# Attention scores of two column blocks written in one run of six products into one piece of two PSUM banks

## The chip, the cores and the metric

The kernel runs on one core of one Trainium2 chip. The metric is the device time of one execution in microseconds; the time given for a kernel is the median of its timed runs.

## What is computed

One layer of an encoder with a convolution branch and an attention branch, over 16 meta tokens and two batches of 512 and 1024 tokens, 1024 features, 16 heads of 64. All inputs are fp32. Cut to what matters here:

```python
u = rms_norm(h, pre_g)
z = einsum('bld,de->ble', u, w_in)            # c_val, c_glu, c_gate, q, k, v, a_gate
conv_out = conv_module(c_val, c_glu, ...) * silu(c_gate)
o_meta, o_grid = neighbourhood_attention(q, k, v, ..., rel_bias)
att = concat([o_meta, o_grid]) * silu(a_gate)
y = einsum('ble,ed->bld', concat([conv_out, att]), w_out)
out = h + rms_norm(y, post_g)
```

The attention is over a window: a token grid 64 columns wide is cut into column blocks, and each query sees 8 rows by 16 columns of keys and the meta keys, with a bias for the relative position. Of each query row the kernel computes the scores, adds bias and mask, takes the softmax and the weighted sum of the values.

## The kernel before

Each fp32 operand of a large matrix product is split into a high and a low part (names with h and l, or hi and lo), and a product is made of three: high by high, high by low, low by high.

**Stages.** First `prenorm` and the projections of the values and of the convolution branch, while VectorE runs the convolution taps (L272). Then the attention loop (L687): `groups` holds 8 head pairs `p`, 3 row groups `g` and 2 halves `hf`, 48 in all. One round `n` writes `scores` of group n, `weighted` of group n-2, `transposes` of group n-1 and `between`, which writes projections of the next keys, queries and gates (L180) to go between; `statistics` (L648) reduces the convolution output for a layer norm. Behind the loop stand the gate projections `a_gate(6, 7)` (L707): six groups of 24 products, each copied out of PSUM by ScalarE (L342). Then the last stage, the output projection (`product`, L794), whose inputs come from `mix` (L757): loads, two VectorE passes, ScalarE `Silu` (L770, L771), a product by the gate (L772), and the split into `mh` (L773) and `ml` (L774). The weights of that projection are split by `load_wo` (L748, L749).

**The scores.** `scores` (L565) treats four column blocks `jj`. For each it takes a piece `ss` of PSUM, issues three products into it (L578), and VectorE reads the piece once (L585), adding the bias and taking the maximum. Then come the exponential on ScalarE (L589), a reciprocal and a scaling on VectorE. `transposes` (L600) turns the result on TensorE into `tp`, ScalarE copies it to SBUF (L602), and `weighted` multiplies it with the values (L616) into `po`.

**PSUM.** Eight banks: `ps_mm` has three (projections, tiles `mm`), `ps_s` two (`ss`), `ps_t` two (`tp`), `ps_o` one (`po`). All are closed before the last stage, and `ps_y` (L711) takes all eight (tiles `py`).

**What sets the order.** The kernel is written through a framework that takes the instructions as they are traced and orders them on each engine with a time model of its own, before anything runs; it places tiles in free buffers and puts in the semaphore waits. Three lines hold parts of that order by hand: `weighted` is issued behind the last score product of the round, the last gates behind the last weighted sum, and the first `mix` behind the last transposed copy, scaling and store:

```python
            with tc.issue_after(last_qk[0].ins):
                weighted(*groups[n - 2])
...
    with tc.issue_after(last_pv[0]):
        for _ in a_gate(6, 7):
...
    with tc.issue_after(last_pt[0]), tc.issue_after(last_norm[0]), tc.issue_after(stores[-2]):
        mix(0, (0,))
```

All transfers are issued on one queue, SyncE's.

Of the kernel before, what the change touches and what calls it, by code (L numbers as in the profile page):

```python
# [10 lines left out]
F32 = mybir.dt.float32  # L11
# [21 lines left out]
GR = (  # L33
    dict(R=9, k3=(0, 11, 0), k2=(0, 16, 0), vrow=0),
    dict(R=12, k3=(8, 12, 0), k2=(8, 16, 0), vrow=8),
    dict(R=13, k3=(13, 13, 0), k2=(10, 16, 3), vrow=13),
)
# [40 lines left out]
BMM, BSS, BTP = 3, 2, 2  # L78
# [15 lines left out]
def tile_encoder(ctx: ExitStack, tc: tile.TileContext, mt, xn, w_main, w_v, wo, cw, cb, lg, lb, pg, postg, rbt, rmask, y):  # L94
    nc = tc.nc
# [9 lines left out]
    const = ctx.enter_context(tc.tile_pool(name="const", bufs=1))  # L105
    es_ps = ExitStack()
    ps_mm = es_ps.enter_context(tc.tile_pool(name="ps_mm", bufs=BMM, space=bass.MemoryType.PSUM))
    ps_s = es_ps.enter_context(tc.tile_pool(name="ps_s", bufs=BSS, space=bass.MemoryType.PSUM))
    ps_t = es_ps.enter_context(tc.tile_pool(name="ps_t", bufs=BTP, space=bass.MemoryType.PSUM))
    ps_o = es_ps.enter_context(tc.tile_pool(name="ps_o", bufs=1, space=bass.MemoryType.PSUM))  # L110

    ones = const.tile([128, 128], F32, name="ones")
    nc.vector.memset(ones, 1.0 / D)
# [317 lines left out]


    es2 = ExitStack()
    kpool = es2.enter_context(tc.tile_pool(name="kpool", bufs=1, side="right", reuse_waits="tile"))
    qpool = es2.enter_context(tc.tile_pool(name="qpool", bufs=1, side="right", reuse_waits="tile"))

# [46 lines left out]
    last_qk = [None]  # L483
# [59 lines left out]
    def block(g, j):  # L543

        e = ebufs[g][{0: 1, 7: 2}.get(j, 0)]
        if g == 0:
            return min(max(j - 1, 0), 5), 3, "k3", 2, 108, e
        R8 = GR[g]["R"] * 8
        if j in (0, 7):
            return min(j, 6), 2, "k2", 2, R8, e  # L550
        return j - 1, 3, "k3", 3, R8, e

    def load_values(p, g):
        esl = slice(p * 128, p * 128 + 128)
        R8 = GR[g]["R"] * 8
        if g == 0:
            vt = apool.tile([108, 2, 6, 128], F32, name="vp", bufs=VPB)
            for ch, p0, b0, k0, n in ((0, 0, 0, 0, 72), (0, 72, 1, 0, 36), (1, 0, 1, 36, 36), (1, 36, 2, 0, 72)):
                nc.sync.dma_start(vt[p0:p0 + n, ch], vd[b0:b0 + 6, k0:k0 + n, esl].rearrange("b k e -> k b e"))
        else:  # L560
            vt = apool.tile([104, 8, 128], F32, name="vt", bufs=2)
            nc.sync.dma_start(vt[:R8], vd[:, GR[g]["vrow"] * 8:GR[g]["vrow"] * 8 + R8, esl].rearrange("b k e -> k b e"))
        vts[p, g] = vt

    def scores(p, g, hf):  # L565
        if hf == 0:
            load_values(p, g)
        kh, kl = kbufs[p]
        qh, ql = qbuf.pop((p, g, hf))
        R8 = GR[g]["R"] * 8  # L570
        for jj in range(4):
            j = hf * 4 + jj
            b0, nk, key, _, _, e = block(g, j)
            ra, rn, ro = GR[g][key]
            w = rn * 8
            ss = ps_s.tile([128, 512], F32, name="ss")
            for i, (q, k) in enumerate(((qh, kh), (qh, kl), (ql, kh))):
                last_qk[0] = nc.tensor.matmul(ss[:, :nk * w], lhsT=q[:, jj].rearrange("p h x -> p (h x)"),  # L578
                                 rhs=k[:, b0:b0 + nk, ra:ra + rn, :].rearrange("p b r c -> p b (r c)"),
                                 start=(i == 0), stop=(i == 2))  # L580
            sv_ = ss[:, :nk * w].rearrange("p (k x) -> p k x", k=nk)[:, :, ro * 8:ro * 8 + R8]
            pt = apool.tile([128, 312], F32, name="pt", bufs=PTB)
            pv = pt[:, :nk * R8]
            sm = apool.tile([128, 4], F32, name="sm", bufs=8)
            nc.vector.tensor_tensor_reduce(out=pv.rearrange("p (k x) -> p k x", k=nk), in0=sv_,  # L585
                                           in1=e.rearrange("p k r c -> p k (r c)"), scale=1.0,
                                           scalar=-3.0e38, op0=ALU.add, op1=ALU.max, accum_out=sm[:, 0:1])
            nc.vector.tensor_scalar(out=sm[:, 1:2], in0=sm[:, 0:1], scalar1=-1.0, scalar2=None, op0=ALU.mult)  # L588
            last[0] = nc.scalar.activation(out=pv, in_=pv, func=AF.Exp, bias=sm[:, 1:2], scale=1.0, accum_out=sm[:, 2:3])  # L589
            nc.vector.reciprocal(sm[:, 3:4], sm[:, 2:3])  # L590
            last_norm[0] = nc.vector.tensor_scalar(out=pv, in0=pv, scalar1=sm[:, 3:4], scalar2=None, op0=ALU.mult).ins  # L591
            pts[p, g, j] = pv
# [94 lines left out]
    for n in range(len(groups) + 2):  # L687
        if n < len(groups):
            p, g, hf = groups[n]
            if (g, hf) == (0, 0) and p > 0:  # L690
                e_build(p)
            scores(p, g, hf)
        if n == len(groups) + 1:
            next(rest)
        if n >= 2:
            with tc.issue_after(last_qk[0].ins):
                weighted(*groups[n - 2])
        if n == len(groups):
            next(rest)
        if 0 <= n - 1 < len(groups):  # L700
            transposes(*groups[n - 1])
        if n < len(groups):
            between(p, g * 2 + hf)
        if n >= STAT0:
            next(stats, None)
# [206 lines left out]
```

## Time and profile before

| | |
|---|---|
| timed runs | 1452.44, 1453.23, 1454.35 us; median 1453.23 |
| the profiled execution | 1453.64 us, of which the span from first to last instruction is 1451.4 |
| TensorE busy | 1434.7 us, 99% of the span |
| VectorE, ScalarE, GpSimdE busy | 70%, 39%, 18% |
| chain of waits that ended last | TensorE 96% |
| attention loop (first score product to the last gates) | 647.7 to 1143.9 us of the span |
| last gates; output projection | 1143.9 to 1177.0; 1177.0 to 1445.4 us |

TensorE's rows in the timeline overlap, since products are pipelined and their ends are modelled. The time that a product takes is read from the start of its row to the start of the next one, not from the duration in the row.

### The profile page before, as it was taken

The page shows a single profiled execution, that of the slowest core. Times are in us where ns is not written, and L with a number is a line of the kernel's source. Part 1 is how long each engine was busy: PE and PEld are TensorE (multiplying, and loading weights), DVE is VectorE, ACT ScalarE, POOL GpSimd, SP SyncE. Part 2 cuts the span into 40 slices and gives each one's busy share as a digit, 9 for nine tenths or more (in the row PEclk, how much of TensorE's full clock was granted, in tenths as well). Part 3 has the DMA queues.
Part 4 walks back from the last instruction along what each step waited for, and adds up shares of the span by engine and source line. Part 5 has one row for each costly group of instructions (what it writes and reads, how often), then busy time and mean ns, then how long its engine had stood idle before and what let it go on. Part 6 is the DMA issues. An engine that isn't in the chain of part 4 may idle for free.

```text
span 1451.4 us, 24134 instructions
## 1 busy us (share of the span) xinstructions
PE 1434.7 (99%) x9536; PEld 1238.8 (85%) x9536; DVE 1012.5 (70%) x1739; ACT 563.5 (39%) x1299; POOL 255.8 (18%) x188
## 2 busy tenths in 40 slices
PE   7999999999999999999999999999999999999998
PEld 6988998988998888888888888888888888888886
DVE  5699999998999899935776677777644373423331
ACT  7312111111111111135555555555554475445540
POOL 2042013102111221121111111111201002221220
PEclk9999999999999999999999999999999999999999
DMA  8113213312231222251232323322332684545441
GB/s 265 47 42 113 59 54 113 90 44 82 84 94 41 77 76 91 80 139 46 74 99 73 90 80 90 95 66 84 80 68 75 206 285 133 166 128 161 131 131 50
DMA packets 153464, 145.19 MB, mean 100 GB/s; under 512 B 37216, under 2 KB 125432, under 8 KB 153352
## 3 DMA queue, kind: packets, MB, share of 16 engines
q1 hardware_dynamic: 153352, 143.67, 33.1%
q8 instruction: 74, 1.21, 0.4%
q14 instruction: 38, 0.31, 0.1%
HBM read 105.35 MB, written 42.72 MB: 102 GB/s over the span
## 4 chain that ended last, share of the span: by engine, by line
PE 96%; POOL 1%; DVE 1%; DMA 1%; ACT 1%; issue 0%; DVEq 0%; SPq 0%; ACTq 0%; POOLq 0%
PE mm L180 39%; PE py L794 18%; PE tp L180 9%; PE mm L322 6%; PE ss L578 5%; PE po L180 5%; PE po L616 4%; PE tp L600 4%; PE tp L322 3%; POOL vl L142 1%; PE po L322 1%; PE ss L202 0%; DMA gb<-in_pg 0%; PE tp L202 0%; PE mm L664 0%; DMA wraw<-in_w_main 0%
## 5 line engine op out<-in xcount | busy, mean ns | idle before, releaser
L180 PE MATMUL mm<-uw,whi 128*128 128x512 f32 (+2 forms) x1904 | 559.8, 371 | 0.0
L272 DVE SCALAR_TENSOR_TENSOR z<-ub,cw_sb,z 128x1536 f32<-128x1536 f32 (+2 forms) x270 | 498.7, 1854 | 8.1
L180 PEld LDWEIGHTS mm<-uw,whi 128*128 128x128 f32 x1904 | 341.8, 188 | 55.2 <-issue 1.3
L180 PE MATMUL mm<-uw,wlo 128*128 128x512 f32 (+2 forms) x952 | 352.3, 370 | 1.1 <-POOL wlo L142 1.1
L142 POOL TENSOR_TENSOR wlo<-wraw,whi 128x1024 fp32r<-128x1024 f32 x48 | 129.5, 2699 | 526.5 <-ACT whi L141 502.7
L180 PEld LDWEIGHTS mm<-uw,wlo 128*128 128x128 f32 x952 | 179.0, 188 | 27.3 <-POOL wlo L142 1.4
L794 PE MATMUL py<-uw,mh 128*128 128x512 f32 x576 | 180.9, 395 | 0.0
L180 PE MATMUL tp<-uw,whi 128*128 128x512 f32 (+2 forms) x512 | 132.9, 344 | 0.0
L794 PEld LDWEIGHTS py<-uw,mh 128*128 128x128 f32 x576 | 108.1, 188 | 25.4
L589 ACT ACTIVATE pt<-pt,sm 128x216 f32<-128x216 f32 (+4 forms) x192 | 97.3, 507 | 80.1 <-DVE sm L588 70.8
L794 PE MATMUL py<-uw,ml 128*128 128x512 f32 x288 | 113.3, 394 | 0.0
L602 ACT COPY pT<-tp 108x256 f32<-108x256 f32 (+4 forms) x192 | 78.2, 420 | 83.8 <-PE tp L600 52.6
L767 DVE TENSOR_TENSOR mx<-mx,mb 128x1024 f32<-128x1024 f32 x12 | 16.1, 1340 | 120.8 <-DMA mx<-zs 120.8
L180 PEld LDWEIGHTS tp<-uw,whi 128*128 128x128 f32 x512 | 89.3, 188 | 11.6
L585 DVE CUSTOM_DVE_ANT_0 pt<-ss,ei 128x216 f32<-128x216 f32 (+2 forms) x144 | 62.6, 437 | 45.4 <-PE ss L578 22.9
L180 PE MATMUL tp<-uw,wlo 128*128 128x512 f32 (+2 forms) x256 | 88.1, 344 | 0.0
L774 POOL TENSOR_TENSOR ml<-mx,mh 128x1024 fp32r<-128x1024 f32 x20 | 48.5, 2441 | 216.4 <-ACT mh L773 216.4
L600 PE MATMUL tp<-ident,pt 128*96 128x128 f32 (+2 forms) x480 | 85.5, 275 | 0.3 <-ACT pT L602 0.2
L322 PE MATMUL mm<-vh,uw 128*128 128x256 f32 x448 | 84.6, 289 | 0.2 <-ACT uw L205 0.2
L591 DVE TENSOR_SCALAR pt<-pt,sm 128x216 f32<-128x216 f32 (+4 forms) x192 | 71.7, 373 | 4.9
L141 ACT CAST whi<-wraw 128x1024 fp32r<-128x1024 f32 x48 | 50.3, 1047 | 61.1 <-DMA wraw<-in_w_main 18.6
L180 PE MATMUL po<-uw,whi 128*128 128x512 f32 (+2 forms) x272 | 72.9, 347 | 0.0
(170 smaller groups left out, 2174.0 us busy)
## 6 DMA issues: line engine op xcount, KB each, us to landing
wraw<-in_w_main SPq DMA_DIRECT2D x48, 512.0 KB
xt<-in_xn SPq DMA_DIRECT2D x12, 512.0 KB
vd<-vs SPq DMA_DIRECT2D x96, 64.0 KB
zs<-zc SPq DMA_DIRECT2D x24, 256.0 KB
cgd<-ag SPq DMA_DIRECT2D x24, 256.0 KB
agd<-ag SPq DMA_DIRECT2D x24, 256.0 KB
ag<-zs SPq DMA_DIRECT2D x24, 256.0 KB
mad<-mo SPq DMA_DIRECT2D x24, 256.0 KB
```

What stands on the lines that cost most here:

```text
L142: eng.tensor_tensor(out=lo, in0=raw, in1=hi.bitcast(F32), op=ALU.subtract)
L180: last_mm[0] = nc.tensor.matmul(ps[:, :n], lhsT=w[:, dc, :], rhs=u[dc // 4][:, dc % 4, :], start=(dc == 0 and i == 0), stop=(dc == DC - 1 ...
L272: nc.vector.scalar_tensor_tensor(out=zv, in0=ub[:, a:b, k:k + 512], scalar=cw_sb[:, c, k:k + 1], in1=zv, op0=ALU.mult, op1=ALU.add)
L322: nc.tensor.matmul(ps[:, :256], lhsT=u[dc // 4][:, dc % 4, :], rhs=w[dc // 4][:, dc % 4, :], start=(dc == 0 and i == 0), stop=(dc == DC - ...
L578: last_qk[0] = nc.tensor.matmul(ss[:, :nk * w], lhsT=q[:, jj].rearrange("p h x -> p (h x)"), rhs=k[:, b0:b0 + nk, ra:ra + rn, :].rearrange ...
L585: nc.vector.tensor_tensor_reduce(out=pv.rearrange("p (k x) -> p k x", k=nk), in0=sv_, in1=e.rearrange("p k r c -> p k (r c)"), scale=1.0, ...
L589: last[0] = nc.scalar.activation(out=pv, in_=pv, func=AF.Exp, bias=sm[:, 1:2], scale=1.0, accum_out=sm[:, 2:3])
L591: last_norm[0] = nc.vector.tensor_scalar(out=pv, in0=pv, scalar1=sm[:, 3:4], scalar2=None, op0=ALU.mult).ins
L600: nc.tensor.transpose(out=tp[:kt, k * 128:k * 128 + 128], in_=pv[:, k * kt:k * kt + kt], identity=ident)
L602: last_pt[0] = nc.scalar.copy(out=pT[:kt, :nt * 128], in_=tp[:kt, :nt * 128]).ins
L616: last_pv[0] = nc.tensor.matmul(po[hs, j, :], lhsT=v, rhs=pT[:kt, k * 128 + h * 64:k * 128 + h * 64 + 64], start=(k == 0), stop=(k == nt - ...
L794: nc.tensor.matmul(pss[hf], lhsT=m[e // 8][:, e % 8], rhs=w[e][:, hf * 512:hf * 512 + 512], start=(n == 0 and i == 0), stop=(n == 15 and i ...
```

## The change

The six products of two neighbouring column blocks are issued together into one tile `sss` of two banks, and each half is then read by VectorE as before. The number and the shapes of the products stay the same, and so do all other instructions. The pool of `ss` is opened last, so that it can be closed behind the first stages, and its two banks become the one piece of the new pool `ps_ss`. Line numbers behind the edit move by up to 8: L578 is L582, L600 is L608, L616 is L624, L794 is L802 and so on.

```diff
     ps_mm = es_ps.enter_context(tc.tile_pool(name="ps_mm", bufs=BMM, space=bass.MemoryType.PSUM))
-    ps_s = es_ps.enter_context(tc.tile_pool(name="ps_s", bufs=BSS, space=bass.MemoryType.PSUM))
     ps_t = es_ps.enter_context(tc.tile_pool(name="ps_t", bufs=BTP, space=bass.MemoryType.PSUM))
     ps_o = es_ps.enter_context(tc.tile_pool(name="ps_o", bufs=1, space=bass.MemoryType.PSUM))
+    es_st = ExitStack()
+    ps_s = es_st.enter_context(tc.tile_pool(name="ps_s", bufs=BSS, space=bass.MemoryType.PSUM, reuse_waits="tile"))
...
     es2 = ExitStack()
+    es_st.close()
+    ps_ss = es_ps.enter_context(tc.tile_pool(name="ps_ss", bufs=1, space=bass.MemoryType.PSUM, reuse_waits="tile"))
...
         for jj in range(4):
             j = hf * 4 + jj
+            if jj % 2 == 0:
+                sss = ps_ss.tile([128, 2, 512], F32, name="sss")
+                for y in range(2):
+                    b0, nk, key, _, _, e = block(g, j + y)
+                    ra, rn, ro = GR[g][key]
+                    for i, (q, k) in enumerate(((qh, kh), (qh, kl), (ql, kh))):
+                        last_qk[0] = nc.tensor.matmul(sss[:, y, :nk * rn * 8], lhsT=q[:, jj + y].rearrange("p h x -> p (h x)"),
+                                                      rhs=k[:, b0:b0 + nk, ra:ra + rn, :].rearrange("p b r c -> p b (r c)"),
+                                                      start=(i == 0), stop=(i == 2))
             b0, nk, key, _, _, e = block(g, j)
             ra, rn, ro = GR[g][key]
             w = rn * 8
-            ss = ps_s.tile([128, 512], F32, name="ss")
-            for i, (q, k) in enumerate(((qh, kh), (qh, kl), (ql, kh))):
-                last_qk[0] = nc.tensor.matmul(ss[:, :nk * w], lhsT=q[:, jj].rearrange("p h x -> p (h x)"),
-                                 rhs=k[:, b0:b0 + nk, ra:ra + rn, :].rearrange("p b r c -> p b (r c)"),
-                                 start=(i == 0), stop=(i == 2))
+            ss = sss[:, jj % 2]
```

The framework orders the changed program anew. Up to the first score product TensorE's order is the same. Behind it the rows move on every engine. Three places:

TensorE in the attention loop, before, at a border of two rounds (tiles: `ss` scores, `po` weighted sums, `tp` transposes, `mm` projections):

```order
L578 MATMUL ss<-kh,ql_5181 128x256
L616 MATMUL po<-pT,vp 64x64 x16
L600 MATMUL tp<-ident,pt 96x128
L578 MATMUL ss<-kh,qh_5186 128x256
L578 MATMUL ss<-kl,qh_5186 128x256
L578 MATMUL ss<-kh,ql_5187 128x256
L180 MATMUL mm<-uw,whi 128x512
L180 MATMUL mm<-uw,wlo 128x512
```

The same round after the change, from the second product of its first block of columns on (`ones` is the small product of `statistics`):

```order
L582 MATMUL sss<-kl,qh_5190 128x256
L582 MATMUL sss<-kh,ql_5191 128x256
L582 MATMUL sss<-kh,qh_5190 128x312
L608 MATMUL tp<-ident,pt 96x128 x3
L582 MATMUL sss<-kl,qh_5190 128x312
L582 MATMUL sss<-kh,ql_5191 128x312
L181 MATMUL mm<-uw,whi 128x512
L181 MATMUL mm<-uw,wlo 128x512
L181 MATMUL mm<-uw,whi 128x512
L672 MATMUL mm<-cw_sb,ones 128x128
L608 MATMUL tp<-ident,pt 96x128 x6
L582 MATMUL sss<-kh,qh_5190 128x312
```

Before, a round's first three products stood alone behind the weighted sums. Now two blocks stand together, here with three transposes between, and the next run of six needs the same piece of PSUM after three projection products, one small product and six transposes.

ScalarE at the end of the last gates, before: from the last six `Silu` passes over the first convolution input to the copy of the sixth and last gate product (`gt` gates, `uw` weights of the output projection, `ag` gate copies; DMAHW are the transfers' semaphores):

```order
L770 ACTIVATE mx<-mx,lb_sb,lg_sb 128x128 x6
L771 ACTIVATE gt<-gt 128x1024 [waits DMAHW1_49]
L748 CAST uw<-xr 128x1024
L748 CAST uw<-yo 128x1024
L773 CAST mh_12158<-mx_12153 128x1024 [waits DVE_49]
L748 CAST uw<-wraw 128x1024 [waits DMAHW4_49]
L771 ACTIVATE gt_12154<-gt_12154 128x1024 [waits DMAHW5_49]
L342 COPY ag<-mm 128x512 [waits DMAHW1_49,PE_49,Activation_49]
L748 CAST uw<-wraw 128x1024 [waits DMAHW7_49]
L773 CAST mh_12159<-mx 128x1024 [waits DVE_49]
L771 ACTIVATE gt<-gt 128x1024 [waits DMAHW0_49]
L342 COPY ag<-mm 128x512 [waits DMAHW6_49,PE_49]
```

The same stretch after the change; ahead of it stand the copy of the fourth gate product and the eight passes of L778:

```order
L779 ACTIVATE gt<-gt 128x1024
L779 ACTIVATE gt_12062<-gt_12062 128x1024 [waits DMAHW1_49]
L756 CAST uw<-wraw 128x1024 [waits DMAHW3_49]
L756 CAST uw<-xr 128x1024
L756 CAST uw<-yo 128x1024
L756 CAST uw<-wraw 128x1024 [waits DMAHW4_49]
L343 COPY ag<-mm 128x512 [waits DMAHW0_49,PE_49,Activation_49]
L781 CAST mh_12067<-mx 128x1024 [waits DVE_49]
L781 CAST mh_12066<-mx_12061 128x1024 [waits DVE_49]
L779 ACTIVATE gt<-gt 128x1024 [waits DMAHW6_49]
L779 ACTIVATE gt_12062<-gt_12062 128x1024 [waits DMAHW7_49]
L343 COPY ag<-mm 128x512 [waits DMAHW5_49,PE_49]
```

In both orders the copy of the last gate product is the last row, with the same kinds of passes ahead of it; now two gate passes that each wait for a transfer stand directly before it.

TensorE at the border of the last gates and the output projection (tile numbers kept), before:

```order
L180 MATMUL mm_12102<-uw_118,wlo_11959 128x512
L180 MATMUL mm_12102<-uw_120,whi_11958 128x512
L794 MATMUL py_12300<-woh0_12184,mh_12148 128x512 [waits Activation_49]
L794 MATMUL py_12300<-wol0_12185,mh_12148 128x512 [waits DVE_49]
L794 MATMUL py_12300<-woh0_12184,ml0_12161 128x512 [waits DVE_49]
```

And after the change:

```order
L181 MATMUL mm_12010<-uw_118,wlo_11867 128x512
L181 MATMUL mm_12010<-uw_120,whi_11866 128x512
L802 MATMUL py_12208<-woh0_12092,mh_12056 128x512 [waits Activation_49]
L802 MATMUL py_12208<-wol0_12093,mh_12056 128x512 [waits DVE_49]
L802 MATMUL py_12208<-woh0_12092,ml0_12069 128x512 [waits DVE_49]
```

The rows are the same, and the places in PSUM are not. In both programs the first output tile (`py_12300`, `py_12208`) lies in bank 0. The six gate products before it take the three banks of `ps_mm` in turn: before the change banks 0, 2, 1, 0, 2, 1, after it 1, 2, 0, 1, 2, 0. So the last user of bank 0 ahead of the first output tile was the fourth gate product, and is now the sixth, `mm_12010`.

## Rows read from the trace of the kernel before

**Rows 1.** The page: span, TensorE's busy time, its granted clock in 40 slices.

```profile
span 1451.4 us, 24134 instructions
PE 1434.7 (99%) x9536; PEld 1238.8 (85%) x9536; DVE 1012.5 (70%) x1739; ACT 563.5 (39%) x1299; POOL 255.8 (18%) x188
...
PEclk9999999999999999999999999999999999999999
```

**Rows 2.** Chain of waits, its two last pieces: start us, us, what.

```profile
1143.93 33.12 PE mm L180 x144
1177.05 268.34 PE py L794 x1152
```

**Rows 3.** Groups by line, VectorE in the attention loop: busy us, mean ns | idle before.

```profile
L585 DVE CUSTOM_DVE_ANT_0 pt<-ss,ei 128x216 f32<-128x216 f32 (+2 forms) x144 | 62.6, 437 | 45.4 <-PE ss L578 22.9 <-PE tp L600 21.2
...
L660 DVE TENSOR_REDUCE cw_sb<-ag 128x64 f32<-128x512 f32 x48 | 51.2, 1078 | 15.2 <-DMA ag<-zs 13.6 <-PE mm L664 1.5
...
L585 DVE DVE_READ_ACCUMULATOR2_ANT sm<- 128x1 f32 x192 | 15.9, 83 | 0.0
```

**Rows 4.** Timeline of TensorE in the attention loop: start us, us, what.

```profile
800.46 0.49 PE L600 MATMUL tp<-ident,pt 128*96 128x128 f32 x3
800.70 0.48 PE L180 MATMUL mm<-uw,wlo 128*128 128x512 f32 x1
801.02 0.63 PE L180 MATMUL mm<-uw,whi 128*128 128x512 f32 x2
...
849.35 0.40 PE L578 MATMUL ss<-kh,qh 128*128 128x288 f32 x1
849.59 0.29 PE L578 MATMUL ss<-kl,qh 128*128 128x288 f32 x1
849.72 0.29 PE L578 MATMUL ss<-kh,ql 128*128 128x288 f32 x1
850.02 0.50 PE L180 MATMUL mm<-uw,whi 128*128 128x512 f32 x1
```

**Rows 5.** Timeline of ScalarE about the end of the last gates.

```profile
1155.54 0.59 ACT L342 COPY ag<-mm 128x512 f32<-128x512 f32 x1 [3.17 <-PE mm L180]
...
1168.06 1.06 ACT L771 ACTIVATE gt<-gt 128x1024 f32<-128x1024 f32 x1 [2.33 <-DMA gt<-agd]
1169.02 0.57 ACT L342 COPY ag<-mm 128x512 f32<-128x512 f32 x1
...
1171.21 2.42 ACT L770 ACTIVATE mx<-mx,lb_sb,lg_sb 128x128 f32<-128x128 f32 x6
1173.54 1.05 ACT L771 ACTIVATE gt<-gt 128x1024 f32<-128x1024 f32 x1
...
1179.23 0.56 ACT L342 COPY ag<-mm 128x512 f32<-128x512 f32 x1
1179.69 1.05 ACT L748 CAST uw<-wraw 128x1024 fp32r<-128x1024 f32 x1
...
1182.55 0.56 ACT L342 COPY ag<-mm 128x512 f32<-128x512 f32 x1
```

**Rows 6.** Timeline of the SyncE queue in the same stretch.

```profile
1163.22 0.37 SPq L765 DMA_DIRECT2D gt<-agd  x1
```

**Rows 7.** Windows behind the last product: stretch, busy us by engine, granted clock.

```profile
1445.50:1448.00 2.50, 0.00 (x0) 0.00 (x0) 1.83 (x5) 0.89 (x3) 0.00 (x0) 0.99 0.00 0
1448.00:1451.40 3.40, 0.00 (x0) 0.00 (x0) 0.41 (x1) 0.00 (x0) 0.00 (x0) 0.50 0.41 154
```

**Rows 8.** Timeline of TensorE at the program's start.

```profile
14.85 1.91 PE L322 MATMUL mm<-vh,uw 128*128 128x256 f32 x8
16.55 1.05 PE L202 MATMUL ss<-ident,un 128*128 128x128 f32 x4
...
19.14 0.39 PE L322 MATMUL mm<-vh,uw 128*128 128x256 f32 x2
19.37 0.28 PE L322 MATMUL mm<-vl,uw 128*128 128x256 f32 x1
```

## The prediction, written before the change was run

> **What bounds the kernel.** [...] TensorE makes up 96% of the chain of waits too, and the chain's last two pieces [rows 2] are the six last gate products (144 products in 33.12 us, 0.23 each) and the 1152 products of the output projection (268.34 us, 0.23 each), without a gap at 1177.05. So nothing can become faster than the sum of TensorE's own products, which the change leaves alone, except where TensorE waits; and any new wait of TensorE is paid in full, because no later stretch has slack to take it back. The question is thus only where TensorE waits now, and where it will. The timeline of the attention loop answers the first part [rows 4]: a score product of 288 columns follows the one before it after 0.13 us, and at one place the row behind the third product starts after 0.30 instead of 0.13 (849.72 to 850.02), a wait of 0.17. I found some eight waits of 0.1 to 0.3 us between 650 and 1144 us in this view, about 1.5 us in all. That is all that better cover could win there.
>
> **The change, part by part.**
>
> *Same work.* 576 score products before and after, with the same columns. In TensorE's order the runs of score products are 183 before and 124 after, and 68 runs of six stand where 18 stood. A change of kind (scores to transposes and back) costs nothing net: three transposes take 0.24 us to the next row and the projection product behind them 0.32 instead of 0.23, together 0.33, three times 0.11 [rows 4]. Behind the weighted sums a score product takes 0.24 to the next row where the same takes 0.13 inside a run [rows 4], 0.11 more; where a transpose comes first, a part of that may be hidden. Transposes directly behind weighted sums fall from 27 places to 11, so 16 places pay between 0 and 0.11, 0 to 1.8 us; I take half, +0.9. The waits of 1.5 us may go: -1.5. Together the loop changes by -0.6, with the ends -1.5 and +1.8.
>
> *One piece instead of two.* A run of six now needs the whole piece, so both reads of the run before. A read takes 0.437 and 0.083 us on VectorE [rows 3], two take 1.04, and in the built program no product of a run signals before its fifth, so that the first half's read doesn't start early. So 1.04 must fit between the sixth product and the next first one. At the place shown in the order there are three projection products (0.69), a small one (about 0.2) and six transposes (six times 0.11): 1.55 us. The tightest of the 95 places has about 1.1, 14 have less than 2.5, and the middle one has over 4. With VectorE free, all fit, so I take zero; what it costs when it is not free is a rival below.
>
> [...]
>
> *The border to the output projection.* Here is what I expect to decide. The pools lie in another order now, and more, the turn of `ps_mm` is one off: the first output tile takes bank 0, which was last used by the fourth of the six gate products and is now used by the sixth, the very last products ahead of it. So the first output product must wait until ScalarE has copied that sixth gate product out. ScalarE works in the order given, and it is late: in the trace of before the copies of the fifth and sixth gate product start at 1179.23 and 1182.55 [rows 5], 2.2 and 5.5 us after TensorE had ended the gates at 1177.05 [rows 2]. Nobody waited for them. After the change everybody does.
>
> How long? From the copy of the fourth gate product to that of the sixth ScalarE has the same passes in both orders: eight `Silu` passes of 128 columns (six take 2.33 us, from 1171.21 to 1173.54, so 0.39 each), ten passes of 1024 columns (six take 5.69, from 1173.54 to 1179.23, so 0.95 each) and two copies (1179.23 to 1179.69, 0.46 each). That is 3.1 + 9.5 + 0.9 = 13.5 us, and the trace shows just that, 1169.02 to 1182.55 [rows 5]. Two gate products take 48 times 0.23 = 11.0 us, so the copy of the sixth cannot come in time.
> - At least: the copy of the fourth starts 0.57 us after its products, as that of the second did (1155.54, after 1143.93 + 11.04 = 1154.97) [rows 2, 5]. Then the sixth starts -11.0 + 0.57 + 13.5 = 3.1 us after TensorE's end and takes 0.56: a stall of 3.6.
> - As before: the copy of the fourth stands behind a cast that waits for a transfer, as it stood behind a gate pass that waited 2.33 for one, and starts 8.03 before the end (1169.02 against 1177.05). Then the stall is -8.03 + 13.53 + 0.56 = 6.1. I take this value, since the passes ahead of it are the same kind.
> - At most: the two gate passes now stand directly before the copy, and each waits for its own transfer. Such a transfer took 4.84 us from its issue to the pass (1163.22 to 1168.06) [rows 5, 6], and it is issued only when the product at L772 has freed the tile. If that adds 2 us, the stall is 8.1.
>
> *The clock.* [...] At the start of the program, dense products took 1.70/8 = 0.213 us at 14.85 and 0.23/2 = 0.115 at 19.14 [rows 8]. If the low level lasts as long as between those rows, 4.3 us, the loss is 4.3 x (1 - 0.115/0.213) = 2.0. No row shows a fall in mid-program, so the bounds are 0 and 2.0, and I take 2.0, the only row there is.
>
> [...]
>
> *Sum.* -0.6 + 0 + 6.1 + 2.0 = +7.5 against the profiled execution's own 1453.64, which lies 0.4 above the median: 1461.1, or **1461 us** against the median.
>
> **The rivals.**
> 1. *No stall at the border; no change.* The copy of the last gate product is taken earlier, or the place of the first output tile matters less than I think. For it: ScalarE has long idle stretches (39% busy). Against it: the 13.5 us of passes against 11.0 of products. Time: 1453.2 with -1.5 to +1.8, so 1451.7 to 1455. It decides if the copy starts within a microsecond of the last gate product. Chance 0.13.
> 2. *Fewer runs win: faster.* If the 0.11 behind a change of kind is lost at every run and not only behind weighted sums, 59 runs less win 59 x 0.11 = 6.5 us, provided that the border costs nothing: 1446.7. Against it: the sum of three transposes and the product behind them, which shows no loss [rows 4]. With the stall it would be about 1454.5. Chance 0.05.
> 3. *The one piece is the wait.* VectorE is 70% busy, and a pass of `statistics` takes 1.08 us [rows 3]. Where it stands ahead of the reads at one of the 14 tight places, TensorE waits up to 1 us: with half of them 7 us more than my sum, 1468. It decides if at several places in the loop the first score product of a run starts later than the row before it allows. Chance 0.12.
>
> **How the numbers follow.** The stall at the border has 0.70. Its own range is 1455.5 (3.6, no loss of clock, -1.5) to 1465 (8.1, 2.0, +1.8). With the lower part of rival 3 and the upper of rival 1, the range for 8 in 10 is 1454 to 1467. A measurement of this kernel can tell about 0.2%, 2.9 us, from no change. Slower by more than that: my forecast and rival 3, less a little for a short stall, 0.81. Within: rival 1 and a part of rival 2, 0.13. Faster: 0.06.
>
> **What would show it.** In the profile of the changed kernel: a gap on TensorE between the last L181 row and the first L802 row of 4 to 8 us, ended by ScalarE's copy at L343; the copy directly behind two L779 passes; then products with a row distance of about 0.43 us for a few microseconds, with a granted clock below 1 in that stretch; the attention loop as long as before, 496 us to within 2. I am wrong on the border if output products begin within 1 us of the last gate product, and on the loop if score products wait for VectorE at L593.

## The result, and the profile after

Measured beside each other on one chip: **1462.22 us** after the change (median of four runs, 1461.48 to 1465.19), 1452.84 before (four runs, 1452.42 to 1454.35). The ratio is 1.0067, 95% interval 1.0055 to 1.0079: slower by 9.4 us. The forecast was 1461, in 1454 to 1467.

The profiled execution of the changed kernel took 1462.81 us, its span is 1460.7, against 1451.4 before [rows 1]: 9.3 us more. Its page, the same lines as shown of before:

```profile
span 1460.7 us, 24134 instructions
...
PE 1437.1 (98%) x9536; PEld 1241.0 (85%) x9536; DVE 1000.3 (68%) x1739; ACT 564.2 (39%) x1299; POOL 256.4 (18%) x188
...
PEclk9999999999999999999999999999999999999999
```

The page shows only that TensorE's busy time rose by 2.4 us; the other 6.9 us of the longer span it stood still. A slice of the page is 36 us long here, and a granted clock of 0.50 over 4.4 us, shown below, leaves no trace in its row PEclk. The chain of waits tells where the time is lost. Its last piece is the output projection (start us, us, what), which answers to the second line of [rows 2]. The gate products do not stand before it as they did, but two transfers of weights, and between those and the projection (not copied here) passes of ScalarE:

```profile
1153.69 7.16 DMA wraw<-in_wo
1163.27 5.62 DMA wraw<-in_wo
1184.00 270.66 PE py L802 x1152
```

The projection begins 6.95 us later than before (1184.00 against 1177.05) and takes 2.32 us longer (270.66 against 268.34). 6.95 + 2.32 = 9.27: the whole difference of the two spans. (Where nothing waits, the chain lets a piece begin at the end of the row before it, a little late: in the timeline of before the first output product starts at 1176.89.) The timeline of TensorE across that border (start us, us, what; in brackets the idle time and what ended it):

```profile
1176.87 0.39 PE L181 MATMUL mm<-uw,whi 128*128 128x512 f32 x1
1184.00 0.80 PE L802 MATMUL py<-woh,mh 128*128 128x512 f32 x1 [6.74 <-ACT ag L343]
1184.59 0.63 PE L802 MATMUL py<-wol,mh 128*128 128x512 f32 x1
...
1188.01 0.63 PE L802 MATMUL py<-woh,mh 128*128 128x512 f32 x1
1188.43 0.44 PE L802 MATMUL py<-wol,mh 128*128 128x512 f32 x1
1188.71 0.39 PE L802 MATMUL py<-woh,ml 128*128 128x512 f32 x1
1188.94 0.40 PE L802 MATMUL py<-uw,mh 128*128 128x512 f32 x1
```

The last gate product hands over after 0.23 us, at 1177.10; then nothing until 1184.00, a stall of 6.9 us that ScalarE's copy at L343 ends. The ten rows from 1184.59 to 1188.43 are 0.43 us apart, from 1188.71 on it is 0.23. The windows of the same stretch (busy us of PE, PEld, DVE, ACT, POOL, then the granted clock) show the granted clock falling:

```profile
1177.30:1184.00 6.70, 0.00 (x0) 0.00 (x1) 6.39 (x6) 6.70 (x10) 0.00 (x0) 0.83 0.98 305
1184.00:1188.40 4.40, 4.40 (x10) 3.51 (x11) 2.88 (x3) 3.31 (x4) 0.00 (x0) 0.50 1.05 394
1188.40:1195.00 6.60, 6.60 (x30) 5.33 (x29) 5.92 (x6) 2.29 (x3) 0.00 (x0) 0.99 1.09 374
```

The granted clock was 0.83 while TensorE stood, 0.50 in the first 4.4 us of products and 0.99 behind them. ScalarE was busy all through the stall (6.70 of 6.70 us). Its timeline, the answer to [rows 5]:

```profile
1168.90 1.05 ACT L756 CAST uw<-wraw 128x1024 fp32r<-128x1024 f32 x1 [2.81 <-DMA wraw<-in_wo]
1169.86 0.58 ACT L343 COPY ag<-mm 128x512 f32<-128x512 f32 x1
...
1179.11 0.58 ACT L343 COPY ag<-mm 128x512 f32<-128x512 f32 x1
1179.58 1.99 ACT L781 CAST mh<-mx 128x1024 fp32r<-128x1024 f32 x2
1181.48 2.00 ACT L779 ACTIVATE gt<-gt 128x1024 f32<-128x1024 f32 x2
1183.38 0.57 ACT L343 COPY ag<-mm 128x512 f32<-128x512 f32 x1
```

The copies of the fourth, fifth and sixth gate product start at 1169.86, 1179.11 and 1183.38. The sixth ends at 1183.95, and the first output product follows at 1184.00. From the copy of the fourth on ScalarE never stops: the two gate passes at L779 stand directly ahead of the last copy, without waiting for a transfer. The wait that counts lies further back, in the 2.81 us that the cast at 1168.90 waited for its weights.

The loop is as it was. The same stretch of 496 us, first of before and then of after:

```profile
647.00:1143.00 496.00, 495.67 (x4435) 432.13 (x4433) 322.88 (x1190) 272.76 (x788) 73.69 (x80) 1.00 0.29 79
```

```profile
647.00:1143.00 496.00, 495.25 (x4414) 432.32 (x4414) 309.26 (x1190) 273.08 (x788) 72.64 (x80) 1.00 0.29 79
```

TensorE is busy for 495.67 and 495.25 of 496 us, and from the first score product to the first of the last gate products it is 496.1 us in both. No score product waits for VectorE at L593. TensorE's list of waits (engine, line, what it waited for: us in all, times, longest) has of the loop and the border these two lines:

```profile
PE py L802 <- ACT ag L343: 6.7, 1, 6.7
...
PE tp L608 <- ACT pT L610: 0.7, 1, 0.7
```

### The profile page after: what moved, and what is told of

Its sections match the earlier page's. It is cut to its first block, busy times and chain, and to the rows that moved or that the text cites. A ratio compares the mean times of both kernels' runs of the same rounds, so it can differ in the third digit from the quotient of the medians.

```text
span 1460.7 us, 24134 instructions
## 1 busy us (share of the span) xinstructions
PE 1437.1 (98%) x9536; PEld 1241.0 (85%) x9536; DVE 1000.3 (68%) x1739; ACT 564.2 (39%) x1299; POOL 256.4 (18%) x188
## 4 chain that ended last, share of the span: by engine, by line
PE 94%; ACT 2%; DMA 1%; POOL 1%; DVE 0%; issue 0%; SPq 0%; DVEq 0%; ACTq 0%; POOLq 0%
PE mm L181 38%; PE py L802 19%; PE tp L181 9%; PE mm L323 5%; PE sss L582 5%; PE po L181 5%; PE po L624 4%; PE tp L608 4%; PE tp L323 3%; POOL vl L143 1%; PE po L323 1%; DMA wraw<-in_wo 1%; PE ss L203 0%; ACT mx L778 0%; DMA gb<-in_pg 0%; PE mm L672 0%
## 5 line engine op out<-in xcount | busy, mean ns | idle before, releaser
L802 PE MATMUL py<-uw,mh 128*128 128x512 f32 x576 | 180.9, 395 | 0.0
L802 PEld LDWEIGHTS py<-uw,mh 128*128 128x128 f32 x576 | 108.1, 188 | 25.4
L802 PE MATMUL py<-uw,ml 128*128 128x512 f32 x288 | 113.3, 394 | 0.0
L593 DVE CUSTOM_DVE_ANT_0 pt<-sss,ei 128x216 f32<-128x216 f32 (+2 forms) x144 | 60.0, 437 | 77.5 <-PE sss L582 76.7
L181 PEld LDWEIGHTS tp<-uw,whi 128*128 128x128 f32 x512 | 89.4, 188 | 11.6
L608 PE MATMUL tp<-ident,pt 128*96 128x128 f32 (+2 forms) x480 | 81.6, 273 | 0.8 <-ACT pT L610 0.7
L323 PEld LDWEIGHTS mm<-vh,uw 128*128 128x128 f32 x448 | 71.0, 193 | 1.5 <-ACT uw L206 0.7
```

Source lines behind the costliest of these rows:

```text
L181: last_mm[0] = nc.tensor.matmul(ps[:, :n], lhsT=w[:, dc, :], rhs=u[dc // 4][:, dc % 4, :], start=(dc == 0 and i == 0), stop=(dc == DC - 1 ...
L323: nc.tensor.matmul(ps[:, :256], lhsT=u[dc // 4][:, dc % 4, :], rhs=w[dc // 4][:, dc % 4, :], start=(dc == 0 and i == 0), stop=(dc == DC - ...
L608: nc.tensor.transpose(out=tp[:kt, k * 128:k * 128 + 128], in_=pv[:, k * kt:k * kt + kt], identity=ident)
L802: nc.tensor.matmul(pss[hf], lhsT=m[e // 8][:, e % 8], rhs=w[e][:, hf * 512:hf * 512 + 512], start=(n == 0 and i == 0), stop=(n == 15 and i ...
```

## The experiments

The theory: all of the loss lies at the border, in a stall because the first output tile's bank was last used by the last gate product, and in the clock that falls during it. The main rival: the scores themselves cost it, by the single piece or by the runs of six.

**Another bank for the last gate product.** `banks` lists the pools, with the names of their tiles, that the projections take in turn. In the changed kernel, ahead of the last gates:

```
+    banks[:] = 0, ((ps_mm, "mm"),) * 5 + ((ps_t, "tp"),)
     with tc.issue_after(last_pv[0]):
         for _ in a_gate(6, 7):
```

> The changed kernel, scores in runs of six in one piece as they are, but the last of the six gate products lies in a bank of the transposes, so that bank 0, which the first output tile takes, was last used by the third gate product. The order of the instructions on each engine stays. Theory of the border: the gap between the last gate product and the first output product falls from 7.1 to under 0.5 us, no product after it is slow, and the time falls from 1462.2 to about 1453 (1451.5 to 1454.5). Rival, the scores themselves cost it (one piece, runs of six): the time stays at 1461 to 1463. Both by half: about 1457.

Measured: 1453.49 us against 1453.09 before, ratio 1.0002 (0.9993 to 1.0011). The order of the rows on TensorE, ScalarE, VectorE and GpSimdE is that of the changed kernel; only the last 24 gate products and their copy name another tile. The chain again has the products directly behind each other, and the projection takes what it took before:

```profile
1144.58 27.73 PE mm L181 x120
1172.30 5.45 PE tp L181 x24
1177.75 268.34 PE py L803 x1152
```

The copy of the last gate product is as late as in the changed kernel, and nobody waits for it:

```profile
1183.78 0.57 ACT L343 COPY ag<-tp 128x512 f32<-128x512 f32 x1
```

The border theory holds. One bank carries the whole loss, and single piece and runs of six together, as they are in the change, cost and win nothing that can be told from zero (the interval is -1.0 to +1.6 us).

**The bank alone.** In the kernel before:

```
+    banks[:] = 0, ((ps_t, "tp"),) * 2 + ((ps_mm, "mm"),) * 4
     with tc.issue_after(last_pv[0]):
         for _ in a_gate(6, 7):
```

> The kernel before, scores in two pieces as they were, but with the first two gate products in the banks of the transposes, so that the last gate product lies in bank 0, which the first output tile takes. Theory of the border: the first output product waits for ScalarE's copy of the last gate product, which in the trace of before ends at 1183.1 against 1177.05 for the products, so a gap of about 6.3 us, then some ten products at 0.43 us from row to row (about 2 us), and 1461 (1459.5 to 1463). Rival, the scores cost it: 1452 to 1454, whatever the bank.

Measured: 1461.58 us, ratio 1.0058 (1.0045 to 1.0071). TensorE's waits and the last piece of the chain:

```profile
PE py L795 <- ACT ag L342: 4.9, 1, 4.9
```

```profile
1181.07 270.88 PE py L795 x1152
```

With the old scores, and with the old order of rows, the bank alone gives 8.5 of the 9.4 us. The profiled execution is the shortest of the five (1460.19). In it the last gate product handed over at 1176.03, so the stall was 5.0 and not 6.3; the projection took 270.88 - 268.34 = 2.5 longer.

**Fillers in the stall.** In the changed kernel, behind the last gates (`last_ws` holds the last gate's weights):

```
+        fill = ps_t.tile([128, 512], F32, name="tp")
+        for i in range(30):
+            nc.tensor.matmul(fill, lhsT=last_ws[0][0][:, i % 4, :], rhs=last_ws[0][1][:, 4:8, :],
+                             start=(i == 0), stop=(i == 29))
```

> The changed kernel with 30 more products of 512 columns behind the last gate product, into a bank of the transposes; nobody reads them. 30 x 0.227 = 6.8 us, about as long as TensorE waits there (6.9). If the slow products behind the gap come from the gap, they are gone: the first output product still starts about 7 us after the last gate product, the rows behind it 0.23 us apart, and the time is 1462.2 - 2.2 = 1460.0 (1459.3 to 1460.8). If they come from something else (first use of the weights of the output, other traffic), they stay: about 1462.2.

Measured: 1459.92 us, ratio 1.0050 (1.0037 to 1.0062). The timeline at the border:

```profile
1176.97 6.96 PE L721 MATMUL tp<-wlo,whi 128*128 128x512 f32 x30
1184.32 0.50 PE L808 MATMUL py<-woh,mh 128*128 128x512 f32 x1 [0.39 <-ACT ag L345]
1184.65 0.40 PE L808 MATMUL py<-wol,mh 128*128 128x512 f32 x1
1184.89 0.39 PE L808 MATMUL py<-woh,ml 128*128 128x512 f32 x1
```

The first output product starts as late as in the changed kernel, but the products behind it are 0.23 us apart, and the projection takes 268.62 us. So the slow products come from TensorE's standing still. Their price is 2.3 us of the 9.4 by the medians (1462.22 - 1459.92), and 270.66 - 268.62 = 2.0 by the projections of the two profiles.

**Waiting for the fifth copy.** In the changed kernel the first output tile's bank goes to the fifth gate product:

```
+    banks[:] = 0, ((ps_mm, "mm"),) * 2 + ((ps_t, "tp"),) * 2 + ((ps_mm, "mm"),) * 2
     with tc.issue_after(last_pv[0]):
         for _ in a_gate(6, 7):
```

> The changed kernel with the third and fourth gate product in the banks of the transposes, so that the fifth lies in bank 0, which the first output tile takes. In the trace of the changed kernel the fifth copy ends at 1179.69, the last gate product's row at 1177.1. Theory of the border: a gap of 2.6 to 2.8 us ended by a copy at L343, so 1453 + 2.6 = 1455.6 if the clock holds through so short a gap (at the end of the program before it was still 0.99 in the 2.5 us behind the last product), up to 1457.8 if it falls as it did behind the gap of 7.1 us. Rival, the scores cost it: 1461 to 1463.

Measured: 1457.22 us (eleven runs, 1454.29 to 1460.47), ratio 1.0029 (1.0020 to 1.0038). The profiled execution took 1454.87:

```profile
1175.65 0.39 PE L181 MATMUL mm<-uw,whi 128*128 128x512 f32 x1
1178.16 0.50 PE L803 MATMUL py<-woh,mh 128*128 128x512 f32 x1 [2.12 <-ACT ag L343]
1178.49 0.39 PE L803 MATMUL py<-wol,mh 128*128 128x512 f32 x1
```

A stall of 2.3 us (1175.88 to 1178.16), ended by the copy, and the clock holds (1.00 in the window from 1178.00 to 1190.00): one more place where the copy that the bank waits for sets the start. The median lies 2.4 above the profiled execution, which the stall alone doesn't explain, so the kernel ran twice more for a profile:

> The kernel of the experiment with the fifth copy once more, for a second profile: its 11 runs lay between 1454.3 and 1460.5, its profiled one at the lower end (1454.87, a gap of 2.1 us ahead of the output products and no slow product). If this one falls among the longer: the gap is longer, 3 to 5 us, since a cast ahead of that copy waited longer for its transfer, and, past some length between 2.1 and 4.9 us, products at 0.43 us follow. If the gap is again near 2 us and the run long, something else varies.

> The kernel of the experiment with the fifth copy a third time. Two profiles gave gaps of 2.1 and 1.5 us ahead of the output products, no slow product, and 1454.9 and 1454.7; the longer ones of its timed runs showed a mean granted clock of 0.998 or 0.997 against 0.999. If this run is above 1456.5: a gap of 3 to 5 us, because the fifth copy is later, or a gap near 2 us with products at 0.43 us behind it. If it is again below 1455.5, what makes the others longer stays open.

Measured: 1454.66 and 1454.78 us, with 1.5 us of wait at the first output product both times, and no slow products. What makes other executions up to 6 us longer stays open. Their mean granted clock (0.998 and 0.997, against 0.999 in the short ones; in the changed kernel it is 0.996 to 0.997) hints that the clock fell in them, but no profile of such an execution exists.

**Runs of six in two pieces.** In the changed kernel:

```
-    ps_ss = es_ps.enter_context(tc.tile_pool(name="ps_ss", bufs=1, space=bass.MemoryType.PSUM, reuse_waits="tile"))
+    ps_ss = es_ps.enter_context(tc.tile_pool(name="ps_ss", bufs=2, space=bass.MemoryType.PSUM, reuse_waits="tile"))
...
-                sss = ps_ss.tile([128, 2, 512], F32, name="sss")
+                sss = []
                 for y in range(2):
+                    sss.append(ps_ss.tile([128, 512], F32, name="sss"))
...
-            ss = sss[:, jj % 2]
+            ss = sss[jj % 2]
```

> The changed kernel with its runs of six products, but each column block has a piece of its own again (two tiles of one bank from the same pool). With two pieces the turn of the banks comes out as before the change: bank 0 was last used by the fourth gate product. Theory of the border: no gap ahead of the output products, and 1452.5 to 1454.5 as before. Rival, runs of six are what costs: 1460 or more. If runs of six win time that the single piece loses again: below 1452.

Measured: 1452.82 us, ratio 0.9998 (0.9989 to 1.0007). But this kernel does not have the change's 68 runs of six. With two pieces to place, the framework put the rows back: its profile has them on TensorE, ScalarE, VectorE and GpSimdE in the order of the kernel before, with 183 runs of score products, of which 18 have six. At one place:

```profile
915.78 0.29 PE L583 MATMUL sss<-kh,ql 128*128 128x288 f32 x1
915.91 0.60 PE L609 MATMUL tp<-ident,pt 128*96 128x128 f32 x4
916.26 0.36 PE L583 MATMUL sss<-kh,qh 128*128 128x256 f32 x1
```

So the run says nothing on runs of six by themselves; what they win or lose is known only together with the single piece, from the run with the other bank. It does tell what turned the banks. Its pools are opened in the new order, and there is no stall (the last gate products start at 1143.82, the projection directly behind them at 1176.93); so it was not the order of the pools, but the single piece and the order of rows that the framework made for it.

**Less work on ScalarE.** In the changed kernel:

```
-            nc.scalar.copy(out=mh, in_=mx)
+            (nc.vector.tensor_copy if t < 2 else nc.scalar.copy)(out=mh, in_=mx)
```

> The changed kernel with the casts mh<-mx of the first two output row tiles on VectorE instead of ScalarE; TensorE's order and the banks are as in the changed kernel. Between the copies of the fourth and the sixth gate product ScalarE now has eight passes of 1024 columns instead of ten, so 13.5 - 2 x 0.95 = 11.6 us. If ScalarE's own work sets the gap, it falls from 7.1 to about 5.2 us, the output products start slow all the same, and the time falls from 1462.2 to 1460.3 (1459.5 to 1461.2). If a transfer that the casts of the weights wait for sets it: the gap stays at 7 us and the time at 1462.

Measured: 1461.61 us, ratio 1.0059 (1.0045 to 1.0073), 0.6 us less than the change instead of 1.9, and not to be told from it (1.0055 to 1.0079). The profile says why. ScalarE, from the fourth copy to the sixth:

```profile
1168.41 0.59 ACT L343 COPY ag<-mm 128x512 f32<-128x512 f32 x1
1168.90 0.88 ACT L778 ACTIVATE mx<-mx,lb_sb,lg_sb 128x128 f32<-128x128 f32 x2
1170.84 1.05 ACT L756 CAST uw<-wraw 128x1024 fp32r<-128x1024 f32 x1 [1.06 <-DMA wraw<-in_wo]
...
1181.23 0.57 ACT L343 COPY ag<-mm 128x512 f32<-128x512 f32 x1
```

That is 12.8 us: the 11.6 expected, and a cast that now stands between the copies and waits 1.06 for its transfer. The stall fell from 6.9 to 5.5 us (the last gate product hands over at 1176.39, the first output product starts at 1181.85), and the projection took 271.14 - 268.34 = 2.8 longer instead of 2.3. Of the 1.4 us by which the stall is shorter, 0.7 comes from the passes (12.8 instead of 13.5) and 0.7 from an earlier copy of the fourth product, 8.0 us ahead of the end of the gates instead of 7.2; the second moves between executions, as shown below. So taking two passes away shortened the stretch by 0.7 us and not by 1.9: the framework ordered ScalarE's rows anew, and a wait for a transfer took the rest.

**How much room the single piece has.** The kernel with the other bank, each read twice:

```
-            nc.vector.tensor_tensor_reduce(out=pv.rearrange("p (k x) -> p k x", k=nk), in0=sv_,
+            for _ in range(2):
+                nc.vector.tensor_tensor_reduce(out=pv.rearrange("p (k x) -> p k x", k=nk), in0=sv_,
...
```

> The kernel of the experiment with the other bank (single piece, runs of six, no gap at the border; 1453.5), with each read of the scores on VectorE done twice, so 2.1 us for the two halves of a piece instead of 1.04. VectorE's busy time in the loop rises from 309 to about 409 of 496 us. By the room counted in the built order (14 of 95 places under 2.5 us, the tightest 1.1) the score products wait at up to 14 places for up to 1 us: 0 to 7 us in all, 1453 to 1461. If the room is much smaller than counted, at most of the 95 places: up to 1.04 x 95 = 99 us more.

The same edit in the kernel before, with the last two gate products in the banks of the transposes:

> The kernel before (two pieces) with each read of the scores done twice, and the last gate products in banks that the first output tile does not take, so that the border costs nothing. A piece is free after its own two reads, and the other piece lies between: no wait of score products beyond 1 us in all, 1452.5 to 1455. What the run with the single piece takes over this one is the price of the single piece at a VectorE that reads twice as long.

Measured, one run each: 1532.12 us with the single piece, 1476.12 with two. Both expectations missed. TensorE's waits in the loop (engine, line, what it waited for: us in all, times, longest), with the single piece:

```profile
PE sss L582 <- DVE sm L594: 35.5, 33, 2.0
PE tp L609 <- ACT pT L611: 8.5, 13, 1.4
```

and with two pieces:

```profile
PE ss L578 <- DVE sm L586: 8.0, 11, 1.2
PE tp L601 <- ACT pT L603: 1.8, 5, 0.4
```

The output projection begins at 1249.04 with one piece and at 1199.53 with two. The 49.5 us between them are what the single piece and the order made for it cost at reads of about 2.1 us; the waits for the reads make up 35.5 - 8.0 = 27.5 of them. With two pieces the projection begins 21.8 us later than in the run with the other bank (1177.75); the waits of the loop explain about half of that, and the rest was not followed. Then only the second half's read was done twice (`range(1 + jj % 2)`):

> As the run with the single piece and each read twice, but only the read of the second half of a piece is done twice: the halves take about 1.56 us together, between 1.04 (no wait) and 2.1 (33 waits of 1.08 us on average, 35.5 in all). If each of those 33 waits shrinks by 0.52: about 18 us of waits of score products, and an output projection that starts some 18 to 35 us later than in the run with the other bank (1177.6). If the edge is sharper, because the longer reads have also pushed other passes of VectorE: under 10 us.

> As the run with two pieces and each read twice, but only every second read is done twice. There 11 waits gave 8.0 us at 2.1 us for two reads; here at most half of it, under 4 us, and the output projection starts at 1178 to 1190. The difference to the single piece with the same reads is the price of the single piece at 1.56 us.

Measured, one run each: 1469.40 us with the single piece, 1472.53 with two. With one piece the waits are under the 10 us of the sharper edge; with two the expectation missed. The score products' waits, with one piece and with two:

```profile
PE sss L582 <- DVE sm L594: 0.2, 1, 0.2
```

```profile
PE ss L578 <- DVE sm L586: 9.0, 10, 1.5
```

So the score products of the single piece wait 0 us for their reads at 1.04 us of reads, 0.2 at 1.56 and 35.5 at 2.1. That looks like an edge and not a slope, but it isn't shown: the framework ordered each of the four programs anew, so the orders differ by more than the reads, and with two pieces the shorter reads even gave the longer waits (9.0 against 8.0). It shows at the end too: with the single piece and reads of 1.56 the projection begins at 1187.6, and a later product in it waits 2.8 us for `ml` of VectorE.

No kernel of the study is faster than the kernel before: the two without a stall, at 0.9998 and 1.0002, are as fast.

## Why the prediction was right, step by step

- **The border: stall of 6.1.** Right in its place, its cause and its passes; 6.9 was measured. The passes from the copy of the fourth product to that of the sixth took 13.52 us (1169.86 to 1183.38), as forecast from [rows 5]. The part mis-sized is the lead of the fourth copy: 7.2 us ahead of the end of the gates (1169.86 against 1177.10) instead of the 8.03 taken over from before. Of this 0.16 is a reading: the gates of before handed over at 1176.89, and 1177.05 is where the chain's piece begins. The rest moves with the transfer that the cast ahead of the copy waits for. In six executions with ScalarE's passes in this order (the change, the other bank, the fillers, and the fifth copy three times) that wait was 2.81, 2.71, 2.90, 2.57, 2.23 and 2.05 us, and the lead 7.2, 7.3, 7.0, 7.6, 8.2 and 8.3: the longer the wait, the shorter the lead. The extra 2 us of the upper end, gate passes that wait for transfers, did not come.
- **The clock: 2.0.** 2.0 was measured against the projection behind the fillers (270.66 - 268.62), 2.3 by the medians. That the clock would fall in mid-program was the author's estimate: in the windows of before it is low only behind the last product (0.50 [rows 7]). Here it was 0.83 in the stall of 6.9 us, 0.50 from there up to 1188.40 and 0.99 behind it, with products directly behind each other in the last two stretches. That the size came out so well is luck: the 4.3 us of [rows 8], against 4.4 here, lie between two rows that were picked, and do not measure how long products were slow there. By more rows of the same timeline, shown below this list, the four small products at 16.55 [rows 8] took 0.85 us to the next row and those at 18.03 took 0.43: the fast distance was there by 18.03, ahead of the 19.14 to which the 4.3 us count, and products had run since 8.23. Nor does any run show that a low clock made the products slow there (the granted clock is 1.00 in the window from 13.80 to 17.80), so that none shows the term as it was worked out; what the runs showed in its place is slow products behind stalls of 5.0, 5.5 and 6.9 us, at a loss of 2.3, 2.5 and 2.0.
- **The loop: -0.6, between -1.5 and +1.8.** Zero, to a few tenths: from the first score product to the first of the last gate products it is 496.1, 495.8 and 495.9 us in the old order (before, the bank alone, two pieces) and 496.1 and 496.2 in the new one (the change, the other bank). The waits that the list shows there are 0.7 us in all before and after. Neither waits won nor changes of kind lost can be seen apart, and 59 runs fewer are worth nothing that this can tell.
- **One piece: 0.** Right, at the reads of this kernel: with 1.04 us for two reads, TensorE's list of waits has no score product that waits for them. With reads of 2.1 us it has 33 such waits, 35.5 us in all, so a cost of this kind is there when the work in between does not cover the reads.
- **Rival 1, no stall,** fell with the copy that starts 6.3 us behind the last gate product's end (1183.38 against 1177.10). **Rival 2, fewer runs win,** fell with the other bank: the runs are 124 as in the change, the border costs nothing, no score product waits, and 1453.49 was measured where 6.5 us less than before were to be seen. **Rival 3, the single piece waits,** did not happen here. Its mechanism exists: reads twice as long gave 33 waits of up to 2.0 us. Whether 7 us was the right price for it at the reads of this kernel can't be told.
- **The sum:** 7.5 forecast, 9.3 measured between the two profiles. Of the 1.8 between them 0.8 is the stall and 0.6 the loop's gain that did not come. The rest stands in no term: the gates hand over 0.2 later (1177.10 against 1176.89), because the loop began later, and the first output product takes 0.1 longer to the next row behind a wait, with fillers too (0.33 against 0.23). All these errors have one sign; the range was wide enough for their sum.

Rows of TensorE at the start of the program, before the change:

```profile
17.40 0.79 PE L202 MATMUL tp<-ident,un 128*128 128x128 f32 x4
18.03 0.60 PE L202 MATMUL ss<-ident,un 128*128 128x128 f32 x4
18.46 0.60 PE L202 MATMUL tp<-ident,un 128*128 128x128 f32 x4
```

## What to carry to other kernels

An edit to one PSUM pool can change which bank another stage gets: at a border of stages, find for the first tile of the new stage who used its bank last and when that user is copied out, because a copy in a busy engine's queue can be late without anyone having waited for it so far; in the run with the other bank ScalarE's last one started at 1183.78, 6.0 us behind the start of the projection. Move the last tiles before a border into banks that the next stage takes later; here that is one line and the whole of 9 us. Count a stall of TensorE of this length higher than its own length: behind those of 5.0 to 6.9 us slow products cost 2.0 to 2.5 us more. And read from the trace whether an edit made the order that it was meant to make: here one that wrote six products together left them apart.

## What the runs showed of the hardware

- The granted clock fell in mid-program: to 0.50 behind the stall of 6.9 us (1184.00 to 1188.40 in the changed kernel) and behind that of 5.0 (1181.00 to 1186.00 with the bank alone). Behind stalls of 5.0, 5.5 and 6.9 us the output products came 0.43 us apart for some 4.4 to 5.4 us, at a loss of 2.3, 2.5 and 2.0 us against the projection of 268.62 us behind the fillers: the longer stall did not cost more. Behind the stall of 2.3 us with the fifth copy the clock held: 1.00 in the window behind it.

```profile
1178.00:1190.00 12.00, 11.84 (x51) 9.64 (x52) 9.62 (x9) 8.48 (x10) 0.00 (x0) 1.00 1.05 340
```

- Products whose result nobody reads kept the clock at 1.00 through the whole wait, and won 2.3 us by the medians. The window of the fillers:

```profile
1177.00:1184.00 7.00, 6.93 (x31) 5.42 (x29) 6.99 (x7) 7.00 (x9) 0.00 (x0) 1.00 0.97 294
```

- VectorE was busy for 309.26 instead of 322.88 us of the loop with the same 1190 instructions, as the two windows of the loop above show. It goes with the new order: the run in two pieces, which kept the old one, has 323.05. The largest part is the scaling of the scores (71.7 us before, 66.3 after); why it is shorter was not tested. TensorE sets the end, so this won nothing.
